# Accumulating DMAs in place of VectorE subtractions for the weight combinations of two down products

## The chip, the cores and the metric

One core of one Trainium2 chip runs the kernel. The metric is device time in microseconds (us) of one execution, and the median of several runs is compared. The engines are TensorE (PE, with its weight loads shown as PEld), VectorE (DVE), ScalarE (ACT), GpSimd (POOL) and SyncE (SP). SP and POOL issue the DMAs of the stage that matters here.

## The reference, cut to what matters

One encoder layer over x of 1024 positions by 1024 channels in float32: a Fourier token mixer, then a gated MLP with a centred convolution over positions, each with adaLN modulation and a layer norm after it. The change touches the last product, the down projection, and its normalization:

```
u = h @ w_up                                   # 1024 x 5632
u = conv over positions (3 taps) + conv_b
val, gate = u[..., :2816], u[..., 2816:]
y = (gelu(gate) * val) @ w_down                # 1024 x 2816 by 2816 x 1024
x = layer_norm(ALPHA * x + g2 * y) * g + b
```

## The kernel before, in words

The down product is done by a scheme of seven half-size products instead of eight (a Strassen-Winograd form). The activations (tensor `gd` in DRAM, 22 tiles of 128 by 1024) are cut into quarters by output rows and by the contraction, the weights `w_down` into quarters W00, W10, W01, W11 (first digit: half of the contraction, second digit: half of the output columns). The products run in the order 1, 2, 5, 6, 3, 7, 4. Each has six blocks `i`: five of two 128-row tiles of the contraction (512 KB of weights) and one of a single tile. So there are 42 steps (p, i).

In each step both operands, an activation block and a weight block, are split into a high and a low part: ACT copies the block to the rounded type fp32r (L53), DVE subtracts that from the block (L54). PE then does three matmuls for each pair of tiles (L284 to L286). The four output row blocks m of a product stand in four PSUM banks and are added into the tiles C when the product ends (`evac`). For the last product `evac` also finishes the four lower row blocks: DVE L821 to L853 with a reciprocal root on POOL (L830 or L840) between, then the store of the row block. `upper_half`, `upper` and `normed` finish the four upper row blocks during products 7 and 4, and their reciprocal root (L426) and their store (L796) are issued on POOL.

The weight operands are made in place by `comb_w` (DVE, L746): for product 5 W01 - W00 in the buffer of W01, for product 6 W11 - (W01 - W00) in the same buffer, for product 7 that minus W00 in the buffer of W00. For product 4 the block W10 is loaded a second time, into the buffer of W11 (tiles `wd_0r` to `wd_10r`), and is subtracted from product 6's combination.

The activation operands are summed partly by accumulating DMAs, issued on POOL (`add_block`, L735): onto `Sg` for products 6 and 3, onto `gr` for product 7.

SP's and POOL's instructions keep the order in which the program writes them. DVE, ACT and PE are ordered by a planner that simulates a timeline with its own costs. The loop over the 42 steps loads 7 steps ahead, issues `add_block` 5 steps ahead, makes combinations 3 steps ahead, and splits 2 steps ahead. The first, second, third and last block of product 4 don't use the shared operand buffers: their parts go to the buffers in the list `fin` (high parts in W00's buffers, low parts in W01's).

Of the kernel before, what the change touches and what calls it, by code (L numbers as in the profile page):

```python
# [11 lines left out]
ALU = mybir.AluOpType  # L12
# [24 lines left out]
def encoder_layer(ctx: ExitStack, tc: tile.TileContext, I, out: bass.AP):  # L37
    nc = tc.nc
    act, dve, pool, pe, sp = nc.scalar, nc.vector, nc.gpsimd, nc.tensor, nc.sync
# [170 lines left out]
    for t, t4 in pairs:  # L210
# [12 lines left out]
        for i, tt in todo:  # L223
            st = sm.tile([128, 2, 6], F32, tag="st", name=f"sta{tt}")
# [204 lines left out]
    for n_t, t in enumerate((1, 2, 0, 3)):  # L429
# [8 lines left out]
        for h in range(2):  # L438
# [15 lines left out]
            for m in range(2):  # L454
                dve.scalar_tensor_tensor(s_[m][:, hs], pb, (-1.0, 1.0)[m], xr[m][:, hs], ALU.mult, ALU.add,
                                         accum_out=sums[m][:, h : h + 1])
        if n_t == 3:
            l_g2 = ada_load(G2)
        for m in range(2):
# [23 lines left out]
            for q in range(2):  # L483
                pt = bank(6 + q, f"tr{nm}_{q}", (4, 128))
                for b in range(4):
                    k = 4 * q + b
                    pe.transpose(pt[:, b, :], hh[:, 128 * k : 128 * k + 128], ident)
                for b in range(4):
                    k = 4 * q + b
# [184 lines left out]
    NK = NB // 2  # L674
# [8 lines left out]
    def w_load(kh, nh, i, slots=None):  # L683
        k, n = PAIRS[i]
        w = slot((slots or bq[kh, nh])[i], [n, 512], F32, f"wd{kh}{nh}_{k}{'r' if slots else ''}")
        r0 = 128 * (NK * kh + k)
        sp.dma_start(w, I["w_down"][r0 : r0 + 128 * n, 512 * nh : 512 * nh + 512].rearrange("(k p) n -> p k n", p=128))
        Bq[kh, nh, i] = w
# [18 lines left out]
    def load_w(p, i):  # L707
        if p in W_OF:
            w_load(*W_OF[p], i)
        elif p == 4:  # L710
            w_load(1, 0, i, bq[1, 1])

    def load_g(p, i):
        if p == 1:
# [23 lines left out]
    def comb_w(p, i):  # L738
        B = {(kh, nh): Bq.get((kh, nh, i)) for kh in range(2) for nh in range(2)}
        if p in (1, 2):  # L740
            return B[p - 1, 0]
        if p == 3:
            return B[1, 1]
        d, x, y = {5: ((0, 1), (0, 1), (0, 0)), 6: ((0, 1), (1, 1), (0, 1)),
                   7: ((0, 0), (0, 1), (0, 0)), 4: ((1, 0), (0, 1), (1, 0))}[p]
        dve.tensor_tensor(B[d], B[x], B[y], ALU.subtract)  # L746
        return B[d]

    def comb_g(p, i):
        r = raw_g.pop((p, i), None)  # L750
# [1 line left out]
            dve.tensor_tensor(Sg[i], Sg[i], r, ALU.add)  # L752
        return Sg[i] if p in (5, 6, 3) else r

    fin = bq[0, 0] + bq[0, 1]

    n_op = [0]

# [39 lines left out]
    def evac(p, m, x):  # L798
        c0, c1 = C[0][m], C[1][m]
        nm = f"f{p}{m}"  # L800
        if p == 1:
            act.activation(c1[:, L], x, AF.Copy, scale=-1.0)
        elif p == 2:
            dve.tensor_tensor(c0[:, L], c1[:, L], x, ALU.subtract)
        elif p == 5:
            act.activation(c1[:, R], x, AF.Copy)
        elif p == 6:
            dve.tensor_tensor(c1[:, L], x, c1[:, L], ALU.add)
            dve.tensor_tensor(c1[:, R], c1[:, R], c1[:, L], ALU.add)
        elif p == 3:  # L810
            dve.tensor_tensor(c0[:, R], c1[:, R], x, ALU.subtract)
        elif p == 7:
            dve.tensor_tensor(c1[:, R], c1[:, R], x, ALU.subtract)
            dve.tensor_tensor(c1[:, L], c1[:, L], x, ALU.subtract)
        else:
            st = st1[m]
            t = slot((33, 34)[m % 2], [512], F32, f"pg{m}")
            n = 512 // x_parts(m)
            rs = sm.tile([128, 1], F32, tag="rs", name=f"rs{nm}")
            if m in sq_rows:  # L820
                dve.tensor_tensor(t, x[0], g2[:, L], ALU.mult)  # L821
                dve.scalar_tensor_tensor(c1[:, L], t, -1.0, c1[:, L], ALU.mult, ALU.add, accum_out=st[:, 0:1])
                nmu = sm.tile([128, 1], F32, tag="nmu", name=f"nmu{nm}")
                dve.tensor_scalar(nmu, st[:, 0:1], st[:, 1:2], -1.0 / D, ALU.add, ALU.mult)
                ss = sm.tile([128, 1], F32, tag="ss", name=f"ss{nm}")
                junk = cp.tile([128, D], mybir.dt.bfloat16, tag="sel", name=f"junk{nm}")
                act.activation(junk, c1, AF.Square, bias=nmu, accum_out=ss)
                ve = sm.tile([128, 1], F32, tag="ve", name=f"ve{nm}")
                dve.tensor_scalar(ve, ss, 1.0 / D, EPS, ALU.mult, ALU.add)
                pool.tensor_tensor(rs, ve, mhalf, ALU.pow)  # L830
            else:
                for k in range(0, 512, n):
                    dve.tensor_tensor(t[:, k : k + n], x[k // n], g2[:, k : k + n], ALU.mult)
                    dve.tensor_tensor(c1[:, k : k + n], c1[:, k : k + n], t[:, k : k + n], ALU.subtract)
                    dve.bn_stats(st[:, k // n, :], c1[:, k : k + n])
                mv = sm.tile([128, 2], F32, tag="mv", name=f"mv{nm}")
                dve.bn_aggr(mv, st)
                ve = sm.tile([128, 1], F32, tag="ve", name=f"ve{nm}")
                dve.tensor_scalar(ve, mv[:, 1:2], EPS, None, ALU.add)
                pool.tensor_tensor(rs, ve, mhalf, ALU.pow)  # L840
                nmu = sm.tile([128, 1], F32, tag="nmu", name=f"nmu{nm}")
                dve.tensor_scalar(nmu, mv[:, 0:1], -1.0, None, ALU.mult)
            nd = D
            lo, hi = slice(0, nd), slice(nd, D)
            if nd < D:
                nb = sm.tile([128, 1], F32, tag="nb", name=f"nb{nm}")
                E(f"nbt{m}").tensor_tensor(nb, nmu, rs, ALU.mult)
                act.activation(c1[:, hi], c1[:, hi], AF.Identity, scale=rs, bias=nb)
                E(f"ng{m}").tensor_tensor(c1[:, hi], c1[:, hi], ffg[:, hi], ALU.mult)
                E(f"nf{m}").tensor_tensor(c1[:, hi], c1[:, hi], ffb[:, hi], ALU.add)  # L850
            if nd:
                dve.scalar_tensor_tensor(c1[:, lo], c1[:, lo], nmu, ffg[:, lo], ALU.add, ALU.mult)
                dve.scalar_tensor_tensor(c1[:, lo], c1[:, lo], rs, ffb[:, lo], ALU.mult, ALU.add)  # L853
            store(1, m)
# [49 lines left out]

    order = (1, 2, 5, 6, 3, 7, 4)
    steps = [(p, i) for p in order for i in range(NP)]
    ready, early, opnd, loaded, added, prepared, split_n = {}, {}, {}, 0, 0, 0, 0
    TAIL = {3: 2, 7: 2, 4: 4}
    acc, late = None, []
    XL = {(7, 5): (1, 0), (4, 0): (1, 1), (4, 1): (1, 2), (4, 2): (1, 3)}  # L910
# [4 lines left out]
    for n, (p, i) in enumerate(steps):  # L915
        while loaded < min(len(steps), n + 7):
            p_, i_ = steps[loaded]
            if p_ != 5:
                load_w(p_, i_)
            load_g(p_, i_)  # L920
            if p_ == 2:
                load_w(5, i_)
            loaded += 1
        while added < min(len(steps), n + 5):
            add_block(*steps[added])
            added += 1
        if 5 <= n < 5 + NP:
            early[5, n - 5] = comb_w(5, n - 5)
        while prepared < min(len(steps), n + 3):
            st_ = steps[prepared]  # L930
            ready[st_] = comb_g(*st_), early.pop(st_) if st_ in early else comb_w(*st_)
            prepared += 1
        if (p, i) in UL:
            xu_load(*UL[p, i])
        if (p, i) in U0:
            upper_half(U0[p, i], 0)
        if (p, i) in XL:
            x_load(*XL[p, i])
        if i == 0:
            acc = [[xbank(f"o{p}_{m}{c}")[:, : 512 // n] for c in range(n)]  # L940
                   for m, n in enumerate(x_parts(m) if p == 4 else 1 for m in range(4))]
            late = []
        if (p, i) == (7, 1):
            ffg = slot(25, [D], F32, "ffg")
            sp.dma_start(ffg, I["ffn_g"])
            ffb = slot(26, [D], F32, "ffb")
            sp.dma_start(ffb, I["ffn_b"])
        if p == 4 and 0 <= i - 1 < 4:
            lower(i - 1)
        while split_n < min(len(steps), n + 2):  # L950
            opnd[steps[split_n]] = operands(*steps[split_n], ready.pop(steps[split_n]))
            split_n += 1
        late.append((PAIRS[i], opnd.pop((p, i))))
        if (p, i) in U1:
            upper_half(U1[p, i], 1)
            upper(U1[p, i])
        tail = TAIL.get(p, 0)
        if i < NP - max(tail, 1):
            todo, final = [late.pop()], False
        elif i == NP - 1:  # L960
            todo, final = late, True
        else:
            continue
        for m in range(4):
            ms = slice(128 * m, 128 * m + 128)
            w = 512 // len(acc[m])
            for c, a in enumerate(acc[m]):
                cs = slice(w * c, w * c + w)
                for (k, kn), (gh, gl, wh, wl) in todo:
                    for q in range(kn):  # L970
                        hl3(a, gh[:, q, ms], gl[:, q, ms], wh[:, q, cs], wl[:, q, cs], k + q == 0, k + q == NK - 1)
            if final:
                evac(p, m, acc[m] if p == 4 else acc[m][0])
# [105 lines left out]
```

## Time and profile before

| | |
|---|---|
| median of 3 runs | 871.85 us (869.87 to 873.02) |
| profiled execution | 872.16 us, span 870.4 us, mean granted clock 0.974 |
| busy in the span | PE 798.9 us (92%), DVE 720.4 (83%), ACT 387.8 (45%), POOL 312.9 (36%) |
| DMA | 131.02 MB, mean 151 GB/s |

The span goes from the first to the last instruction on the core; 1.76 us of the profiled execution lie outside it. Busy shares are means over stages with different limits, so the stage of the change, roughly from 620 us on, is read by itself below.

### The profile page before, as it was taken

The page shows a single profiled execution, that of the slowest core. Times are in us where ns is not written, and L with a number is a line of the kernel's source. Part 1 is how long each engine was busy: PE and PEld are TensorE (multiplying, and loading weights), DVE is VectorE, ACT ScalarE, POOL GpSimd, SP SyncE. Part 2 cuts the span into 40 slices and gives each one's busy share as a digit, 9 for nine tenths or more (in the row PEclk, how much of TensorE's full clock was granted, in tenths as well). Part 3 has the DMA queues.
Part 4 walks back from the last instruction along what each step waited for, and adds up shares of the span by engine and source line. Part 5 has one row for each costly group of instructions (what it writes and reads, how often), then busy time and mean ns, then how long its engine had stood idle before and what let it go on. Part 6 is the DMA issues. An engine that isn't in the chain of part 4 may idle for free.

```text
span 870.4 us, 10731 instructions
## 1 busy us (share of the span) xinstructions
PE 798.9 (92%) x3943; PEld 644.0 (74%) x3943; DVE 720.4 (83%) x991; ACT 387.8 (45%) x559; POOL 312.9 (36%) x244
## 2 busy tenths in 40 slices
PE   2699799998979999999999999999999989999990
PEld 1466577877858888888888888888878868887880
DVE  6972857899899999998888888888677795556998
ACT  7442514577454344444444444444454324335612
POOL 4776802498355444334343333431000122301102
PEclk9899899999989999999999999999999999999995
DMA  9658665572112212322212222210598886808703
GB/s 344 252 183 306 248 228 198 178 270 81 49 49 97 98 73 76 116 85 88 73 72 73 98 97 81 89 49 25 186 375 296 279 213 113 157 25 270 261 27 143
DMA packets 49749, 131.02 MB, mean 151 GB/s; under 512 B 5512, under 2 KB 6664, under 8 KB 49696
## 3 DMA queue, kind: packets, MB, share of 16 engines
q1 hardware_dynamic: 41008, 106.47, 34.6%
q0 software_dynamic: 8400, 22.81, 9.8%
q10 hardware_dynamic: 288, 1.05, 0.3%
q8 instruction: 31, 0.51, 0.2%
q14 instruction: 22, 0.18, 0.1%
HBM read 110.39 MB, written 19.92 MB: 150 GB/s over the span
## 4 chain that ended last, share of the span: by engine, by line
PE 54%; DVE 8%; DMA 7%; issue 3%; POOL 1%; SPq 0%; ACT 0%; DVEq 0%; POOLq 0%
PE x L286 14%; PE x L284 14%; PE x L285 14%; PE o L285 4%; PE o L286 4%; PE o L284 4%; DMA gr<-gd 2%; DMA xu<-x1d 2%; DVE d_1l L54 2%; DMA wd<-in_w_down_dram 1%; DVE d_0l L54 1%; DMA wd_2r<-in_w_down_dram 1%; DMA Sg<-gd 1%; DVE C L853 1%; DVE C L883 1%
## 5 line engine op out<-in xcount | busy, mean ns | idle before, releaser
L284 PE MATMUL x<-Hh,a 128*128 128x512 f32 (+2 forms) x416 | 155.8, 378 | 5.3 <-ACT a L53 5.3
L285 PE MATMUL x<-Hl,a 128*128 128x512 f32 (+2 forms) x416 | 156.6, 377 | 3.9 <-DVE Hl L54 3.1
L286 PE MATMUL x<-Hh,a 128*128 128x512 f32 (+2 forms) x416 | 155.8, 375 | 0.0
L285 PE MATMUL o<-d_1l,d_0h 128*128 128x512 f32 (+1 forms) x299 | 115.0, 385 | 6.5 <-DVE d_1l L54 4.3
L286 PE MATMUL o<-d_1h,d_0l 128*128 128x512 f32 (+1 forms) x299 | 114.7, 384 | 0.0
L284 PE MATMUL o<-d_1h,d_0h 128*128 128x512 f32 (+1 forms) x299 | 102.4, 382 | 0.0
L284 PEld LDWEIGHTS x<-Hh,a 128*128 128x128 f32 x416 | 78.7, 191 | 21.2 <-ACT a L53 6.0
L285 PEld LDWEIGHTS x<-Hl,a 128*128 128x128 f32 x416 | 79.0, 190 | 19.2 <-DVE Hl L54 4.4
L53 ACT ACTIVATE a<-S 128x512 fp32r<-128x512 f32 x80 | 50.4, 630 | 95.6 <-PE x L286 87.2
L286 PEld LDWEIGHTS x<-Hh,a 128*128 128x128 f32 x416 | 78.9, 190 | 14.5 <-issue 0.8
L588 POOL DMA_DIRECT2D gd<-ug x20 | 11.4, 569 | 170.2 <-DVE ug L587 170.2
L285 PEld LDWEIGHTS o<-d_1l,d_0h 128*128 128x128 f32 x299 | 56.6, 189 | 18.7 <-DVE d_1l L54 7.7
L54 DVE TENSOR_TENSOR a<-wu,a 128x512 fp32r<-128x512 f32 x60 | 63.6, 1060 | 3.0 <-ACT a L53 3.0
L286 PEld LDWEIGHTS o<-d_1h,d_0l 128*128 128x128 f32 x299 | 56.6, 189 | 10.8
L284 PEld LDWEIGHTS o<-d_1h,d_0h 128*128 128x128 f32 x299 | 56.3, 189 | 11.0
L54 DVE TENSOR_TENSOR a<-S,a 128x512 fp32r<-128x512 f32 x80 | 61.0, 763 | 0.8
L53 ACT ACTIVATE a<-wu 128x512 fp32r<-128x512 f32 x60 | 37.5, 625 | 40.1 <-PE x L286 38.2
L635 POOL TENSOR_TENSOR S<-wu 128x512 f32<-128x512 f32 x20 | 29.8, 1492 | 69.0 <-DVE a L54 60.3
L735 POOL DMA_DIRECT2D Sg<-gd x12 | 13.9, 1239 | 91.6 <-DVE d_0l L54 91.6
L579 DVE SCALAR_TENSOR_TENSOR t<-uv,cw,t 128x1023 f32<-128x1023 f32 x20 | 35.9, 1793 | 11.4 <-ACT t L578 11.3
L636 POOL TENSOR_TENSOR S<-wu,S 128x512 f32<-128x512 f32 x20 | 43.9, 2195 | 0.1
L53 ACT ACTIVATE d_0h<-Sg 128x1024 fp32r<-128x1024 f32 x15 | 15.9, 1062 | 58.1 <-PE o L285 58.1
(341 smaller groups left out, 1944.5 us busy)
## 6 DMA issues: line engine op xcount, KB each, us to landing
aw<-in_ada_w_dram SPq DMA_DIRECT2D x48, 512.0 KB, 6.2
wu<-in_w_up_dram SPq DMA_DIRECT2D x44, 512.0 KB, 3.2
gd<-ug POOLq DMA_DIRECT2D x20, 512.0 KB, 2.9
wd<-in_w_down_dram SPq DMA_DIRECT2D x20, 512.0 KB, 9.7
gr<-gd SPq DMA_DIRECT2D x15, 512.0 KB, 7.6
gA<-gd SPq DMA_DIRECT2D x10, 512.0 KB, 10.7
Sg<-gd POOLq DMA_DIRECT2D x10, 512.0 KB, 6.2
x<-in_x_dram SPq DMA_DIRECT2D x8, 512.0 KB, 6.1
```

Source lines behind the costliest of these rows:

```text
L53: act.activation(hi, src, AF.Copy)
L54: (eng or dve).tensor_tensor(lo, src, hi, ALU.subtract)
L284: pe.matmul(ps_ap, hi_l, hi_r, start=first, stop=False)
L285: pe.matmul(ps_ap, hi_l, lo_r, start=False, stop=False)
L286: pe.matmul(ps_ap, lo_l, hi_r, start=False, stop=last)
L579: dve.scalar_tensor_tensor(tt[:, 1:S], u[:, 0 : S - 1], w[:, 0:1], tt[:, 1:S], ALU.mult, ALU.add)
L588: pool.dma_start(gd[j], gg)
L635: pool.tensor_tensor(S3, A11, A21, ALU.subtract)
L636: pool.tensor_tensor(S4, A12, S2, ALU.subtract)
L735: pool.dma_start(raw_g[p, i] if p == 7 else Sg[i], gd[k0 : k0 + n, :, 512 * mh : 512 * mh + 512].rearrange("k p c -> p k c"), accum_op=ALU ...
L853: dve.scalar_tensor_tensor(c1[:, lo], c1[:, lo], rs, ffb[:, lo], ALU.mult, ALU.add)
L883: E(f"ub{m}").tensor_tensor(c, c, ffb, ALU.add)
```

## The change

The combinations of products 6, 7 and 4 change sign, and two of the three are no longer made by DVE. Product 6 now takes (W01 - W00) - W11, still a DVE subtraction. Product 7's weights are W00 + that, made by a DMA from SBUF to SBUF that accumulates onto W00's buffer. Product 4's weights are W10 + product 6's combination, made by a DMA from DRAM that accumulates onto W01's buffer. These twelve DMAs are issued on POOL by a new function `add_w`, nine steps ahead, behind the same step's `add_block`. The second load of W10 on SP is dropped, the low parts of product 4's operands go to W11's buffers instead of W01's, and the signs in `evac` follow.

```diff
     def load_w(p, i):
         if p in W_OF:
             w_load(*W_OF[p], i)
-        elif p == 4:
-            w_load(1, 0, i, bq[1, 1])
...
-        d, x, y = {5: ((0, 1), (0, 1), (0, 0)), 6: ((0, 1), (1, 1), (0, 1)),
-                   7: ((0, 0), (0, 1), (0, 0)), 4: ((1, 0), (0, 1), (1, 0))}[p]
+        if p == 7:
+            return B[0, 0]
+        if p == 4:
+            return B[0, 1]
+
+        d, x, y = {5: ((0, 1), (0, 1), (0, 0)), 6: ((0, 1), (0, 1), (1, 1))}[p]
         dve.tensor_tensor(B[d], B[x], B[y], ALU.subtract)
         return B[d]
+
+    def add_w(p, i):
+        if p == 7:
+            pool.dma_start(Bq[0, 0, i], Bq[0, 1, i], accum_op=ALU.add)
+        elif p == 4:
+            k, n = PAIRS[i]
+            r0 = 128 * (NK + k)
+            pool.dma_start(Bq[0, 1, i], I["w_down"][r0 : r0 + 128 * n, 0:512].rearrange("(k p) n -> p k n", p=128),
+                           accum_op=ALU.add)
...
-    fin = bq[0, 0] + bq[0, 1]
+    fin = bq[0, 0] + bq[1, 1]
...
-            dve.tensor_tensor(c1[:, L], x, c1[:, L], ALU.add)
+            dve.tensor_tensor(c1[:, L], c1[:, L], x, ALU.subtract)
...
-            dve.tensor_tensor(c1[:, R], c1[:, R], x, ALU.subtract)
-            dve.tensor_tensor(c1[:, L], c1[:, L], x, ALU.subtract)
+            dve.tensor_tensor(c1[:, R], c1[:, R], x, ALU.add)
+            dve.tensor_tensor(c1[:, L], c1[:, L], x, ALU.add)
...
-                dve.scalar_tensor_tensor(c1[:, L], t, -1.0, c1[:, L], ALU.mult, ALU.add, accum_out=st[:, 0:1])
+                dve.scalar_tensor_tensor(c1[:, L], t, 1.0, c1[:, L], ALU.mult, ALU.add, accum_out=st[:, 0:1])
...
-                    dve.tensor_tensor(c1[:, k : k + n], c1[:, k : k + n], t[:, k : k + n], ALU.subtract)
+                    dve.tensor_tensor(c1[:, k : k + n], c1[:, k : k + n], t[:, k : k + n], ALU.add)
...
+        while added_w < min(len(steps), n + 9):
+            add_w(*steps[added_w])
+            added_w += 1
```

## Rows read from the trace of the kernel before

**Rows 1.** The page's 40 equal slices of the span (21.8 us each), busy tenths of PE and of DVE.

```profile
PE   2699799998979999999999999999999989999990
DVE  6972857899899999998888888888677795556998
```

**Rows 2.** Stretches of the down product: busy us of each engine with its instructions, granted clock, DMA busy share, GB/s.

```profile
720.00:740.00 20.00, 20.00 (x90) 16.57 (x89) 10.68 (x11) 9.02 (x12) 4.69 (x4) 1.00 0.63 103
735.00:775.00 40.00, 40.00 (x178) 33.14 (x177) 22.42 (x24) 15.23 (x16) 8.23 (x7) 1.00 0.57 99
...
785.00:820.00 35.00, 32.89 (x146) 26.89 (x146) 28.40 (x42) 20.93 (x26) 3.65 (x5) 1.00 0.95 315
800.00:820.00 20.00, 20.00 (x91) 16.54 (x90) 20.00 (x30) 13.21 (x18) 2.08 (x2) 1.00 0.97 359
820.00:840.00 20.00, 20.00 (x107) 17.24 (x106) 20.00 (x30) 7.30 (x9) 1.23 (x2) 1.00 0.14 55
840.00:860.00 20.00, 8.23 (x50) 7.19 (x48) 20.00 (x43) 4.86 (x7) 2.58 (x4) 0.81 0.08 33
```

**Rows 3.** The chain of work that ended last, from 600 us on: start, us, what.

```profile
789.37 10.32 DMA wd_2r<-in_w_down_dram
...
858.55 0.57 POOL out_dram L796
859.14 1.13 POOL rsf L830
...
865.40 1.28 DVE C L853
```

**Rows 4.** DVE in order of time around the start of product 7: start, us, line, operation, tiles, shape, and in brackets the idle time before it and what ended it.

```profile
791.72 0.69 DVE L866 SCALAR_TENSOR_TENSOR C<-xu,C 128x512 f32<-128x512 f32 x1 [2.69 <-DMA xu<-x1d]
...
795.78 1.23 DVE L746 TENSOR_TENSOR wd_0r<-wd,wd_0r 128x1024 f32<-128x1024 f32 x1 [3.11 <-DMA wd_0r<-in_w_down_dram]
796.92 1.22 DVE L54 TENSOR_TENSOR d_0l<-gr,d_0h 128x1024 fp32r<-128x1024 f32 x1
798.06 1.22 DVE L54 TENSOR_TENSOR d_1l<-wd,d_1h 128x1024 fp32r<-128x1024 f32 x1
...
799.71 1.23 DVE L746 TENSOR_TENSOR wd_2r<-wd,wd_2r 128x1024 f32<-128x1024 f32 x1 [0.37 <-DMA wd_2r<-in_w_down_dram]
```

**Rows 5.** The instructions of the line that makes the combinations, L746: duration in ns as minimum, median and maximum, first and last start.

```profile
L746 DVE TENSOR_TENSOR wd<-wd,wd x18: 684/1220/1229, 643.7 to 721.1; 128x1024 f32<-128x1024 f32 x15, 128x512 f32<-128x512 f32 x3
...
L746 DVE TENSOR_TENSOR wd_0r<-wd,wd_0r x1: 1226/1226/1226, 795.8 to 795.8; 128x1024 f32<-128x1024 f32 x1
...
L746 DVE TENSOR_TENSOR wd_10r<-wd,wd_10r x1: 684/684/684, 819.2 to 819.2; 128x512 f32<-128x512 f32 x1
```

**Rows 6.** PE in order of time: the first matmul behind its gap in product 7, and its last matmul of the kernel.

```profile
799.33 0.50 PE L285 MATMUL o<-d_1l,d_0h 128*128 128x512 f32 x1 [2.11 <-DVE ve_fn L424]
...
847.96 0.28 PE L286 MATMUL o<-d_1h,d_0l 128*128 128x256 f32 x1
```

**Rows 7.** DVE in order of time during product 4: the last combination, the split behind it, and the first work on the last row block of the last product.

```profile
819.22 0.68 DVE L746 TENSOR_TENSOR wd_10r<-wd,wd_10r 128x512 f32<-128x512 f32 x1
819.83 1.22 DVE L54 TENSOR_TENSOR d_0l<-gA,d_0h 128x1024 fp32r<-128x1024 f32 x1
...
851.01 0.73 DVE L833 TENSOR_TENSOR pg<-o,g 128x256 f32<-128x256 f32 x2
```

**Rows 8.** POOL in order of time: its accumulating DMAs (L735) and the stores of the first two upper row blocks (L796).

```profile
733.46 1.19 POOL L735 DMA_DIRECT2D Sg<-gd  x1 [6.97 <-DVE d_0l L54]
...
744.34 2.12 POOL L735 DMA_DIRECT2D Sg<-gd  x2 [4.25 <-DVE d_0l L54]
745.63 5.74 POOL L735 DMA_DIRECT2D gr<-gd  x4
...
791.63 0.91 POOL L735 DMA_DIRECT2D gr<-gd  x1 [6.52 <-DMA gr<-gd]
...
811.12 0.61 POOL L796 DMA_DIRECT2D out_dram<-C  x1 [11.13 <-DVE C L883]
...
826.01 0.59 POOL L796 DMA_DIRECT2D out_dram<-C  x1 [10.68 <-DVE C L883]
```

**Rows 9.** ACT in order of time: the split of product 3's single block, the next split, the first split of product 7, and the last weight split of product 4.

```profile
755.55 0.63 ACT L53 ACTIVATE d_0s<-Sg 128x512 fp32r<-128x512 f32 x1 [0.94 <-PE o L286]
...
760.76 1.06 ACT L53 ACTIVATE d_0h<-Sg 128x1024 fp32r<-128x1024 f32 x1 [4.06 <-PE o L285]
...
777.08 1.06 ACT L53 ACTIVATE d_0h<-gr 128x1024 fp32r<-128x1024 f32 x1 [3.43 <-PE o L285]
...
833.15 0.62 ACT L53 ACTIVATE d_1h<-wd_10r 128x512 fp32r<-128x512 f32 x1
```

**Rows 10.** SP's queue in order of time: the last activation loads of product 7 (six issues, the last one at 787.3) and the first second load of W10.

```profile
704.86 82.80 SPq L695 DMA_DIRECT2D gr<-gd  x6
...
788.39 0.42 SPq L687 DMA_DIRECT2D wd_0r<-in_w_down_dram  x1
```

**Rows 11.** The accumulating DMAs of `add_block`, L735: time on POOL in ns as minimum, median and maximum, first and last start, and the time from issue to landing.

```profile
L735 POOL DMA_DIRECT2D Sg<-gd x12: 1188/1197/1422, 684.3 to 745.0; - x12
L735 POOL DMA_DIRECT2D gr<-gd x6: 909/2329/3604, 745.6 to 791.6; - x6
...
DMA to landing us min/median/max: 5.4/6.8/14.8
```

More of the change, by code (lines that the diff above doesn't have):

```diff
@@ L906, in encoder_layer @@
     steps = [(p, i) for p in order for i in range(NP)]
-    ready, early, opnd, loaded, added, prepared, split_n = {}, {}, {}, 0, 0, 0, 0
+    ready, early, opnd, loaded, added, added_w, prepared, split_n = {}, {}, {}, 0, 0, 0, 0, 0
     TAIL = {3: 2, 7: 2, 4: 4}
```

## The prediction

> **What bounds the kernel now.** I read the page's slices first. PE is full nearly everywhere and DVE is far from full in most of the down product, but in the last slices it turns round: PE falls to nothing while DVE still stands at 9 [rows 1]. The table of stretches makes that sharp. From 720 to 775 us PE has no gap and DVE idles for close to half of the time; from 800 to 860 us DVE is busy for 60 of 60 us, and from 840 on PE has only 8.23 us of work [rows 2]. PE's last matmul ends at 848.2 us [rows 6], and DVE's last instruction ends 18.4 us later, at 866.7 [rows 3]; the store of the row block fills the remaining 3.7 us of the span. The chain of waits says the same: in its last stretch it goes through DVE, back to a 10.32 us DMA of the reloaded W10 at 789.37 [rows 3]. So in this stage PE is the limit up to about 790 us and DVE from there to the end. Work taken from DVE counts only if it is taken behind 790.
>
> **The change part by part.** *Product 7's combinations off DVE.* Of the 18 combinations that ended by 722.3 us [rows 5], six belong to product 7. Their removal is worth nothing: what DVE is spared there it has as idle time right behind, and between 720 and 775 us PE never waits [rows 2].
>
> *Product 4's combinations off DVE.* Five of 1.22 us and one of 0.68 [rows 5], between 795.8 and 819.9. Successive DVE instructions overlap a little, so I count the distance to the next start: 795.78 to 796.92 is 1.14 [rows 4], and 819.22 to 819.83 is 0.61 [rows 7]. That makes 5 x 1.14 + 0.61 = 6.3 us, all in a stretch where DVE is the limit. This is the main term.
>
> *The second load of W10 off SP's queue.* Its first block can't be issued before 788.39, behind the last of product 7's activation loads, which wait for their buffers [rows 10]. With it go the two waits of DVE on it, 3.11 and 0.37 us [rows 4], together 3.5. Behind the first one stood the split of product 7's third block, which ended at 799.2 for a PE that had run dry: its gap of 2.11 us [rows 6] goes too, so PE's last matmul moves to about 846.1. How much of the 3.5 DVE keeps is open. From 792.7 it has the two splits of that block, 2.3 us, and then needs activation blocks and residual rows that are loaded in a stretch where the DMA engines are 0.95 busy [rows 2]. It can be all, if these come in time, or nothing, if another arrival blocks DVE in the same place, as the residual row did for 2.69 us just before [rows 4]. I take half, 1.7.
>
> *The buffers.* Low parts of product 4's first blocks no longer wait for later combinations to give up W01's buffers: the third block's split stands right behind the last combination now [rows 7]. W11's buffers are free once product 3 is split, so this only helps; I count nothing, because DVE was busy all that time.
>
> *The signs* cost nothing: the same instructions on the same tiles.
>
> *Twelve more DMAs on POOL.* The nearest rows are the accumulating DMAs that are there: 1.20 us of POOL's time for those onto Sg, up to 3.60 for those onto gr, landing in 5.4 to 14.8 us, 6.8 in the median [rows 11]. By order of issue, product 7's six start behind the accumulation at 733.46 and alternate with `add_block`'s; product 4's first two follow among those of 745.63, the third just ahead of the accumulation at 791.63, the fourth behind it [rows 8]. The fifth stands behind the first upper row block's store (811.12) and the sixth behind the second's (826.01) [rows 8], since `upper` is written between them.
>
> What the DMA engines need: from 720 to 740 us, where accumulations make the traffic, 0.63 x 20 = 12.6 us of all engines moved 103 x 20 = 2.06 MB [rows 2], so about 3.2 us for each 512 KB. Product 7's six (5.5 blocks) want 17.6 us and product 4's first two 6.4. From 735 to 775 the engines are busy for 0.57 x 40 = 22.8 us [rows 2]; with 24 more they are full and spill over 775 a little. Who waits? Product 3's single block: its activations, accumulated last in the group at 744.34 [rows 8], now stand behind three weight accumulations. I put its landing at 736 + 5.5 x 3.2 + 3.6 (the median landing less the transfer) = 757. ACT wants it at 755.55, and its next split is due at 760.76 with some 2 us to spare before PE notices [rows 9]. That holds. Product 7's first block is wanted at 777.08 [rows 9] and its eight transfers (7.5 blocks) end near 764. Both ends: a transfer inside SBUF might cost as little as no time beside the others, which changes nothing, or several times 3.2 us, which is the slower rival below.
>
> The last ones: the sixth lands at 826.6 + 1.2 + 6.8 = 834.6 even if the store comes no earlier than now, and the split that wants it stands at 833.15 before and is followed by a DVE backlog [rows 9]. The store should come earlier, so I count nothing.
>
> **The sum.** 872.16 (the profiled execution) - 6.3 - 1.7 = 864.2. The median of the runs is 0.3 below the profiled one, so I forecast 864.0. The lower bound of this case is all 3.5 plus the 2.69, 872.16 - 6.3 - 3.5 - 2.7 = 859.7; the upper bound is the 6.3 less what the order takes back, in the first rival.
>
> **The rivals.** *PE's end holds DVE.* DVE's order is planned. If it keeps its place for the last row block, whose second half starts at 851.4 now [rows 7], DVE can't pass PE's last matmul: at 846.1 that is a gain of 5.3, 866.9; at 848.2, if PE's gap stays, 3.1, 869.1. Against it speaks that of the 15.3 us of DVE behind 851.4 only some 4.3 belong to the last row block; the rest can be put before it.
>
> *A fuller gain.* If the planner finishes three row blocks before PE ends, what is left is the last one's chain of some 4.3 us and a store of 3.7: a span of 854, 856 in all. DVE's remaining work speaks against it: 795.8 to 866.7 less some 0.7 of idling and the 6.3 is 64 us, and from 792.7 on it ends near 856.7 even without idling, which gives a span of 860.4 and 862.
>
> *No change.* The reciprocal roots of the lower row blocks are issued on POOL behind all four upper stores: 858.55, 859.14, then DVE [rows 3]. The fifth and sixth accumulations now stand in that chain. If it isn't shortened by the relief of DVE, its two issues cost 2 x 1.2 = 2.4, 874.6, and at 3.6 us each 7.2, 879.4. For it speaks that the chain's last links stand on the path now; against it, that most of its length is waiting for DVE.
> The Trainium skill speaks for a high price (SBUF — State Buffer, section "SBUF: two separate sides"): descriptors of a DMA issued on GpSimd are written by it, and it is shut out of a shared port while DVE runs in its two-port modes; the page's section "A bandwidth-pool intuition that's wrong (but worth ruling out)" has such a DMA take about 3100 ns instead of 620. By that ratio an issue of 1.2 us would be an estimated 6, and 9.6 us more on this chain. The trace doesn't bear it out: the accumulations onto Sg never took over 1.42 us [rows 11].
>
> *Slower: transfers inside SBUF are dear.* At c us for each 512 KB, product 3's single block lands at 747.6 + 3c. PE waits once that passes about 762.5, c = 5; the gain of 8 is used up at c = 7.6 and at three times the row, 9.6, PE is 14 late and the kernel takes about 878. Nothing in the trace shows such a transfer.
>
> **How the numbers follow.** The forecast (861 to 867) 0.54; PE's end holds DVE (867 to 869.2) 0.17; a fuller gain (856 to 861) 0.08; no change 0.12; slower 0.09. A measurement tells about 0.3% from no change, 2.6 us: below 869.2 is faster, above 874.5 slower. So faster 0.79, same 0.12, slower 0.09. The range that leaves out about 2 in 10 is 858.5 to 870.5.
>
> **What would show it.** Right: DVE's combinations of product 4 gone between 795 and 820, no PE gap near 797, PE's last matmul at 845 to 847, DVE's last instruction at 857 to 861, the stores of the upper rows several us earlier. Wrong: PE idle between 756 and 790 behind a split of product 3 or 7 that waits for a DMA; DVE idle for many us behind 793; POOL issues of 3 us and more behind 800; or the last two weight splits of product 4 waiting for their accumulation, with PE idle behind 830.

## The result, and the profile after

The changed kernel takes 867.57 us in the median of six runs (866.47 to 868.73), against 871.8 for the kernel before (869.87 to 873.95, six runs). The ratio is 0.995, with a 95% interval of 0.9937 to 0.9963: a gain of 4.2 us, about half of the 7.8 that were forecast (871.8 - 864.0), and inside the range. The profiled execution took 866.72 us, of which the span is 864.9 (before: 872.16 and 870.4).

The page's 40 slices, PE and DVE, of the changed kernel:

```profile
PE   2699799997979999999999999999999989999990
DVE  6972857899899999998888888888677784556897
```

Nearly every digit is what it was [rows 1]: at the end of DVE's row only 9 became 8 in the 38th slice (800 to 822 us) and 8 became 7 in the last. Slices of 21.6 us are too coarse for a gain of 4. The table of stretches, changed kernel: length, then the busy us and instructions of PE, PE's weight loads, DVE, ACT and POOL, the granted clock, the DMA engines' busy share and GB/s. The share adds up the times of the packets that start in the stretch, so it can pass 1.

```profile
785.00:820.00 35.00, 35.00 (x157) 28.80 (x156) 26.35 (x41) 21.91 (x26) 8.77 (x9) 1.00 1.01 302
820.00:840.00 20.00, 19.68 (x102) 16.76 (x101) 20.00 (x32) 4.41 (x6) 1.32 (x2) 1.00 0.13 32
725.00:780.00 55.00, 55.00 (x245) 45.54 (x244) 30.14 (x33) 19.57 (x21) 17.42 (x16) 1.00 0.88 161
783.00:861.33 78.33, 60.99 (x298) 51.16 (x296) 68.82 (x113) 32.50 (x40) 17.73 (x17) 0.91 0.58 175
```

And two stretches of the kernel before that answer to the last two; the second runs from the start of product 7 (to within 0.1 us of its first matmul) to DVE's end, as 783.00 to 861.33 does after.

```profile
725.00:780.00 55.00, 55.00 (x244) 45.57 (x243) 29.13 (x32) 21.92 (x26) 10.62 (x9) 1.00 0.49 84
785.36:866.68 81.32, 60.76 (x298) 51.03 (x296) 74.61 (x119) 32.73 (x40) 10.66 (x13) 0.91 0.52 181
```

The last pair holds most of the account. Behind the start of product 7, DVE has six instructions fewer and 74.61 - 68.82 = 5.8 us less to do. But the stretch became only 81.32 - 78.33 = 3.0 us shorter, because DVE's idle time grew from 6.7 to 9.5 us. Of the relief, 2.8 us went into new waiting, although the waits for the reloaded W10 are gone.

The spans differ by more, 5.5 us, because product 7 starts 2.4 us earlier in this execution. Of that, 1.8 us is there at the first matmul of the down product already. PE in order of time, before:

```profile
629.23 0.39 PE L284 MATMUL o<-d_1h,d_0h 128*128 128x512 f32 x1
```

and after:

```profile
627.39 0.39 PE L284 MATMUL o<-d_1h,d_0h 128*128 128x512 f32 x1
```

Up to there both programs give every engine the same instructions in the same order, so these 1.8 us are not the change's. Another 0.5 us comes up between that matmul and product 7, where a PE gap in product 5 is shorter (3.25 us, before 3.88), and 0.15 in the last store. Without the 1.8 the two profiles differ by 3.7 us, which fits the 4.2 of the medians (interval 3.2 to 5.5).

Where DVE waits now: DVE in order of time, changed kernel (in brackets the idle time before the instruction and what ended it).

```profile
785.45 1.22 DVE L54 TENSOR_TENSOR d_1l<-wd,d_1h 128x1024 fp32r<-128x1024 f32 x1
792.01 0.69 DVE L877 SCALAR_TENSOR_TENSOR C<-xu,C 128x512 f32<-128x512 f32 x1 [5.35 <-DMA xu<-x1d]
...
804.06 0.69 DVE L877 SCALAR_TENSOR_TENSOR C<-xu,C 128x512 f32<-128x512 f32 x1 [0.75 <-DMA xu<-x1d]
...
847.48 0.74 DVE L844 TENSOR_TENSOR pg<-o,g 128x256 f32<-128x256 f32 x2
```

DVE's waits by what ended them, changed kernel from 782 us on: us in total, times, the longest.

```profile
DVE C L877 <- DMA xu<-x1d: 6.1, 2, 5.3
DVE nbfn L891 <- POOL rs_fn L426: 1.1, 3, 0.5
DVE C L893 <- ACT C L892: 1.0, 1, 1.0
```

The waits for the reloaded W10 (3.11 and 0.37, together 3.5) went, but the wait for the residual row ahead of them, 2.69 before [rows 4], is 5.35 now, 2.7 more. The rest of the idle time, 6.7 - 2.7 - 3.5 = 0.5 us before, is 9.5 - 5.35 = 4.1 us now, in small waits of under 1 us each: for another residual row, for POOL's reciprocal roots, for ACT. So 3.5 went and 6.3 came. SP's queue and POOL hold a possible reason. SP, changed kernel:

```profile
785.63 0.33 SPq L797 DMA_DIRECT2D xu<-x1d  x1
```

POOL in order of time, changed kernel:

```profile
781.43 1.19 POOL L733 DMA_DIRECT2D gr<-gd  x1 [24.80 <-DVE C L876]
782.13 1.71 POOL L757 DMA_DIRECT2D wd<-in_w_down_dram  x1
791.45 0.88 POOL L733 DMA_DIRECT2D gr<-gd  x1 [7.61 <-DMA gr<-gd]
...
807.33 0.61 POOL L807 DMA_DIRECT2D out_dram<-C  x1 [7.72 <-DVE nmufu L881]
...
817.29 0.61 POOL L807 DMA_DIRECT2D out_dram<-C  x1 [6.83 <-DVE C L894]
```

And before, POOL and SP:

```profile
783.91 1.19 POOL L735 DMA_DIRECT2D gr<-gd  x1 [32.54 <-DMA gr<-gd]
...
788.00 0.33 SPq L786 DMA_DIRECT2D xu<-x1d  x1
```

The residual row's load is issued 2.4 us earlier than before (785.63, where it was 788.00), but two accumulations were issued 3.5 and 4.2 us ahead of it, where before there was one, 4.1 us ahead; and it takes 6.4 us to arrive instead of 3.7, counted to the DVE instruction that it releases. So the row comes at 792.0 in the one kernel and at 791.7 in the other: DVE reaches its place earlier and waits longer. That the accumulations ahead are the cause was a reading of order at this point; the experiments take it up.

### The profile page after: what moved, and what is told of

Read it like the earlier page. It is cut to its first block, busy times and chain, and to the rows that moved or that the text cites. A ratio compares the mean times of both kernels' runs of the same rounds, so it can differ in the third digit from the quotient of the medians.

```text
span 864.9 us, 10742 instructions
## 1 busy us (share of the span) xinstructions
PE 799.9 (92%) x3943; PEld 644.2 (74%) x3943; DVE 708.3 (82%) x979; ACT 387.3 (45%) x559; POOL 328.9 (38%) x256
## 4 chain that ended last, share of the span: by engine, by line
PE 57%; DVE 6%; DMA 6%; issue 2%; POOL 1%; ACT 1%; SPq 0%; POOLq 0%; ACTq 0%; DVEq 0%
PE x L286 14%; PE x L284 14%; PE x L285 14%; PE o L285 5%; PE o L286 5%; PE o L284 5%; DMA gr<-gd 2%; DMA xu<-x1d 2%; DMA wd<-in_w_down_dram 1%; DVE d_1l L54 1%; DVE d_0l L54 1%; DMA Sg<-gd 1%; DVE C L864 1%; POOL S L635 0%; DVE C L894 0%
## 5 line engine op out<-in xcount | busy, mean ns | idle before, releaser
L54 DVE TENSOR_TENSOR d_1l<-wd,d_1h 128x1024 fp32r<-128x1024 f32 (+1 forms) x37 | 44.0, 1189 | 0.0
```

The source lines that it names most:

```text
L54: (eng or dve).tensor_tensor(lo, src, hi, ALU.subtract)
```

## The experiments

Five questions: which of the two products brings the gain (the first two runs and a mended one); what DVE's relief and the spared load are worth each by itself (three runs); whether the residual row took the missing half (two); whether the late accumulations did (two); and whether a plain earlier load would have done as well as an accumulation (two). All ratios are against the kernel before, run beside them (medians 871.49 to 871.91).

**Product 7's part alone.** Product 4 goes back to a second load of W10 and DVE's combination (with the sign that goes with the negated W01), and its low parts go to W01's buffers.

```
 load_w:  +        elif p == 4:
          +            w_load(1, 0, i, bq[1, 1])
 comb_w:  -        if p == 4: return B[0, 1]
          +        4: ((1, 0), (0, 1), (1, 0)) with ALU.add
 add_w:   only p == 7
```

> The changed kernel, but product 4's weights are made as before: W10 is loaded a second time and DVE adds product 6's combination; only product 7's weights come from the accumulating DMAs inside SBUF. Theory A (the gain comes from product 4's six DVE instructions, which stood where DVE sets the end; product 7's stood where DVE has idle time): no gain, 870.5 to 872.5 us against some 871.8 for the kernel before. Rival B (product 7's part carries the gain, since DVE is relieved before product 6 too): 868 us or below. Rival C (the transfers inside SBUF cost something that product 4's part had to pay for): 873 us or above.

871.15 us; ratio 0.9995 (0.9981 to 1.0009). Product 7's combinations come off DVE where DVE idles, and it is worth nothing, as costed.

**Product 4's part alone, first form.** Product 7 is combined on DVE again.

```
 comb_w:  -        if p == 7: return B[0, 0]
          +        7: ((0, 0), (0, 1), (0, 0)) with ALU.add
 add_w:   only p == 4
```

> The changed kernel, but product 7's weights are made by DVE as before (an addition, the signs are the changed kernel's); only product 4's come from accumulating DMAs. Theory A: the whole gain, 866.5 to 868.5 us. Rival B (product 7's part carries it): 870 to 872 us. Rival C (the transfers inside SBUF cost something): under 866 us.

884.11 us; ratio 1.0146 (1.0126 to 1.0165). A miss, and by the way the kernel was written: each accumulation onto W01's buffer stands ahead of the DVE combination of product 7 that reads the same buffer, so that combination takes W01 with W10 already added, and has to wait for the DMA. Four of product 7's six combinations waited; DVE in order of time:

```profile
761.09 1.23 DVE L746 TENSOR_TENSOR wd<-wd,wd 128x1024 f32<-128x1024 f32 x1 [6.12 <-DMA wd<-in_w_down_dram]
...
797.86 1.22 DVE L746 TENSOR_TENSOR wd<-wd,wd 128x1024 f32<-128x1024 f32 x1 [4.71 <-DMA wd<-in_w_down_dram]
...
825.44 1.23 DVE L746 TENSOR_TENSOR wd<-wd,wd 128x1024 f32<-128x1024 f32 x1 [3.12 <-DMA wd<-in_w_down_dram]
...
827.78 0.69 DVE L746 TENSOR_TENSOR wd<-wd,wd 128x512 f32<-128x512 f32 x1 [1.04 <-DMA wd<-in_w_down_dram]
```

This kernel doesn't tell what was asked, but it prices something else: a DVE instruction that stands behind such an accumulation waits for it, 15.0 us in four waits here, and with it all of DVE's queue. The change has no such place, because nothing on DVE but a split reads an accumulated block.

**Product 4's part alone, mended.** As above, with the accumulations written behind the combinations:

```
-        while added_w < min(len(steps), n + 9): ...   (ahead of the prepared loop)
+        while added_w < min(len(steps), n + 9): ...   (behind it)
```

> Product 7's weights by DVE, product 4's by accumulating DMAs, as in e2_p4_only, but with each accumulation written behind the making of product 7's combination, so that DVE's addition no longer waits for a DMA and reads the buffer before W10 is added. Theory A: the whole gain of the change, 866.5 to 868.5 us. If the transfers inside SBUF (absent here) cost something in the changed kernel: under 866.5 us. If product 7's part is needed for the gain: 869.5 us or above.

869.13 us; ratio 0.9966 (0.995 to 0.9982). With the 0.05% of product 7's part that makes 0.4%, against 0.5% for the change: the two parts add up within their intervals. The time itself lies between the forecasts, 0.6 us above the one for the whole gain. The first residual row, SP and DVE:

```profile
788.97 0.33 SPq L793 DMA_DIRECT2D xu<-x1d  x1
...
795.12 0.69 DVE L873 SCALAR_TENSOR_TENSOR C<-xu,C 128x512 f32<-128x512 f32 x1 [5.10 <-DMA xu<-x1d]
```

The long wait for the residual row is there without the transfers inside SBUF. Product 4's accumulations from DRAM are enough for it.

**DVE's relief alone.** The kernel before with product 4's six subtractions left out; the second load of W10 stays, so product 4 multiplies by W10 instead of the difference.

```
+        if p == 4:
+            return B[1, 0]
```

> The kernel before without product 4's six subtractions: the reloaded block W10 alone stands as its weights, so the output isn't the reference's; all loads and the buffers stay. Theory A (DVE's work is what counts): about the changed kernel's time, 866.5 to 869 us. Rival D (the second load of W10 with its two waits is what counts, 3.5 us of them on DVE): about the kernel before, 870.5 to 872 us, since the weights still arrive as late.

866.38 us; ratio 0.9938 (0.9921 to 0.9954), a gain of 5.1 us, with the load as late as before. The stretch from product 7's start to DVE's end:

```profile
785.80:862.30 76.50, 60.79 (x298) 51.06 (x296) 68.55 (x113) 32.51 (x40) 14.28 (x13) 0.92 0.55 193
```

and DVE's waits:

```profile
DVE C L868 <- DMA xu<-x1d: 3.8, 2, 2.5
DVE d_1l L54 <- ACT d_1h L53: 2.6, 1, 2.6
```

DVE has 68.55 us of work, as after the change, but 8.0 us of idle time instead of 9.5, in a stretch that is 1.8 shorter. The late load still costs DVE 2.6 us, by way of ACT's split of it, and the residual row 2.5. The changed kernel doesn't have the first and pays 5.35 for the second, 2.8 more: as the two traces read, what the spared load gave was lost at the residual row. The two kernels' times differ by 1.2 us (866.38 and 867.57), which their intervals don't settle.

**The spared load alone, first form.** The kernel before without the second load; product 4 subtracts from W11, which is resident, instead.

```
-        elif p == 4:
-            w_load(1, 0, i, bq[1, 1])
-        4: ((1, 0), (0, 1), (1, 0))
+        4: ((1, 1), (0, 1), (1, 1))
```

> The kernel before without the second load of W10: product 4's six subtractions take the block W11 that is in the buffer, so the output isn't the reference's; DVE's work and the buffers stay. Theory A: little, 869.5 to 871.5 us, because the waits of 3.5 us on the load go but DVE still has the 6.3 us. Rival D (the load counts): the changed kernel's time or better, 868.5 us or below.

866.25 us; ratio 0.994 (0.9922 to 0.9958). A miss, and the trace says why. The combinations' line:

```profile
L744 DVE TENSOR_TENSOR wd<-wd,wd x24: 684/1220/1227, 645.0 to 776.5; 128x1024 f32<-128x1024 f32 x20, 128x512 f32<-128x512 f32 x4
```

All 24 combinations are over by 776.5. With its operand resident the planner moved product 4's six ahead of product 7, into DVE's idle time, so this kernel too takes 6 us off DVE where DVE is the limit. It repeats the run before it (0.9938), and says nothing of the load by itself. But it shows that DVE's own combinations, with their operand there early enough, cost no more than leaving them out.

**The spared load alone, second form.** The load is left out and the six subtractions are held back by an operand that comes late: each subtracts the same step's activation block, in place of W10's.

```
-        raw_g[p, i] = g_load(1, 1, i, block(i, (1, 0), "gA22_"))
+        raw_g[p, i] = Bq[1, 0, i] = g_load(1, 1, i, block(i, (1, 0), "gA22_"))
-        4: ((1, 0), (0, 1), (1, 0))
+        4: ((1, 1), (0, 1), (1, 0))
```

> The kernel before without the second load of W10, but with product 4's six subtractions kept in their late place: they subtract the activation block of the same step, which is loaded there anyway, so the output isn't the reference's. Theory A (the place of DVE's work counts, the load by itself little): 869 to 871.5 us. Rival D (the load counts): 867 us or below, like e4_no_load.

870.14 us; ratio 0.999 (0.9976 to 1.0003). DVE in order of time, the first and the last of the six:

```profile
793.86 1.23 DVE L744 TENSOR_TENSOR wd<-wd,gA 128x1024 f32<-128x1024 f32 x1 [1.26 <-DMA gA<-gd]
...
813.17 0.68 DVE L744 TENSOR_TENSOR wd<-wd,gA 128x512 f32<-128x512 f32 x1
```

Now they stand where they stood; the first one waits 1.26 us for the activation block, where it waited 3.11 for W10. The load's absence is worth 0.9 us by the ratio, 1.8 by the medians, 2.1 by the interval's lower end (0.0024 x 871.9), and nothing by its upper one. The 1.7 that the prediction took for it lies inside; so does zero.

**The residual row early.** In the changed kernel, two of the upper half's residual rows are loaded in product 3, ahead of the accumulations, instead of in products 3 and 7.

```
-    UL = {..., **{((7, i) if i else (3, 5)): (i, 1) for i in range(4)}}
+    UL = {..., (3, 2): (0, 1), (3, 3): (1, 1), (7, 2): (2, 1), (7, 3): (3, 1)}
```

> The changed kernel, with the second halves of the residual rows of the upper row blocks 0 and 1 loaded during product 3 (steps (3, 2) and (3, 3)) instead of behind product 7's activation loads. Theory E (what DVE was spared was partly given back as idle time: 5.35 us at 786.7 to 792.0 until that residual row came, and some 3 us until 820 behind the late chain of the upper rows): most of the 5.35 comes back, 861.5 to 864.5 us. Rival F (that idle time costs nothing, because DVE's order is bound by PE's results of product 7 and 4 anyway): 866.5 to 868.5 us, no change against the changed kernel.

865.46 us; ratio 0.9925 (0.9908 to 0.9942): 2.1 less than the change, half of what was hoped. The 5.35 us wait is gone, and another has come into its place. DVE in order of time:

```profile
796.58 0.16 DVE L891 TENSOR_TENSOR nbfn<-nmufu,rs_fn 128x1 f32<-128x1 f32 x1 [3.26 <-POOL rs_fn L426]
```

POOL in order of time, the same kernel:

```profile
793.84 0.88 POOL L733 DMA_DIRECT2D gr<-gd  x1 [7.43 <-DVE d_0l L54]
794.39 1.57 POOL L757 DMA_DIRECT2D wd<-in_w_down_dram  x1
795.12 1.43 POOL L426 TENSOR_TENSOR rs_fn<-ve_fn,mhalf 128x1 f32<-128x1 f32 x1
```

The row block's reciprocal root (L426), whose input DVE had written at 786.7, is issued behind two accumulations on POOL, the first of which waited 7.43 us for a DVE split. DVE, a few instructions on, waits for that root.

**The same edit in the kernel before.**

> The kernel before with the same earlier load of the two residual rows. Theory E: DVE waits 2.69 us for the row before, but 3.11 us for the reloaded weights stand right behind it and are not touched: a gain of 0 to 3, 869 to 872 us. Rival F: no change, 871 to 872.5 us. If it gains as much as in the changed kernel (5 us), the residual row was a limit of its own and the change's relief has nothing to do with it.

869.98 us; ratio 0.9973 (0.9959 to 0.9988). It gains about as much without the change (0.27%) as with it (0.25%). So the residual row is a limit of its own in both kernels, and the part of the missing gain that is the change's doing can't be read from this edit. DVE's wait behind it, for the reload, is 3.5 us there, as before.

**Product 4's accumulations earlier.** Twelve steps ahead instead of nine.

```
-        while added_w < min(len(steps), n + 9):
+        while added_w < min(len(steps), n + (9 if added_w < 36 else 12)):
```

> The changed kernel, with product 4's accumulating DMAs written twelve steps ahead instead of nine, so that none stands behind a store of an upper row block or behind product 7's last activation accumulations on POOL. Theory E: the third one no longer runs beside the residual row's load at 785.6, which landed after 6.3 us instead of 3.7: up to 2.6 us less, and ACT's wait of 1.37 us on the last but one goes: 865 to 867.5 us. Rival G (POOL's queue with the stores sets the end): 863 us or below. If the DMA engines, full from 741 to 775 us, only spill further: 867.5 us or above.

867.73 us; ratio 0.9953 (0.9938 to 0.9968): no gain on the change. DVE's waits from 782 us on:

```profile
DVE C L877 <- DMA xu<-x1d: 7.7, 3, 3.1
```

The first of the three, DVE in order of time:

```profile
790.20 0.69 DVE L877 SCALAR_TENSOR_TENSOR C<-xu,C 128x512 f32<-128x512 f32 x1 [3.12 <-DMA xu<-x1d]
```

With no accumulation issued in the 20 us ahead of its load (786.03), the first residual row arrives after 4.2 us, and the wait for it is 3.1 us instead of 5.35. But the edit moved the activation accumulation of 781.43 as well (to 786.45, behind that load), so by itself it doesn't say which of the two accumulations had lengthened the way. The other traces do. In the five kernels that had only the activation accumulation ahead of that load, by 4.1 to 4.3 us, the row came after 3.6 to 4.2 us: 3.7 in the kernel before, 4.2 with product 7's part alone, 3.6 without the subtractions, 4.0 and 4.1 without the load. In the two that had one of product 4's accumulations 3.5 us ahead too, it came after 6.4 (the change) and 6.2 (product 4's part, mended). So the weight accumulation lengthens the way by some 2 to 3 us. What that costs in time is not shown: two later rows are now waited for by 1.9 and 2.7 us, where the changed kernel has one wait of 0.75, and PE shows gaps of 2.2 and 2.8, so nothing is won in sum. The edit doesn't clear the place either; the sixth weight accumulation now stands there, at 787.17, just ahead of the second row's load (787.41).

**Both edits.**

> The changed kernel with both edits, the residual rows' earlier load and product 4's accumulations twelve steps ahead. If the two cures are independent, the gains add: 860 to 864 us. If both only cure the same wait, no better than the earlier load alone.

864.23 us (862.39 to 865.93); ratio 0.9914 (0.9897 to 0.9931). DVE's waits from 782 us on:

```profile
DVE C L877 <- DMA xu<-x1d: 3.1, 2, 1.8
DVE nbfn L891 <- POOL rs_fn L426: 2.2, 2, 1.8
```

This is the best median: 7.5 us below the kernel before and 3.3 below the change, with intervals that don't touch. From the early rows alone (865.46) it isn't told apart: those intervals overlap. Against the kernel before with the same residual rows early (0.9973), the accumulations are worth 0.59%, 5.1 us, and by the two intervals some 3 to 7. That fits what the relief of DVE alone brought (5.1), as it should with the rows and the accumulations out of each other's way, but it doesn't show that as the cause.

**A plain load, early.** The kernel before; W10's second load is issued at step 28 in one piece, ahead of the next load of activations, and DVE goes on subtracting.

```
-        elif p == 4:
-            w_load(1, 0, i, bq[1, 1])
...
+        if n == 28:
+            for k in range(NP):
+                w_load(1, 0, k, bq[1, 1])
```

> The kernel before, complete, without accumulations onto weights, with W10's second load written on SP ahead of product 7's fifth activation load, so that it arrives from 750 us on and DVE can make product 4's combinations in its idle time before 785. Theory A: DVE is relieved as in the changed kernel, and no accumulation disturbs the loads at 785: 865.5 to 867.5 us, as good as the change or better. If accumulating by DMA is what brings the gain: 870 us or above.

871.26 us; ratio 0.9994 (0.9978 to 1.001): nothing. DVE's waits from 755 us on:

```profile
DVE wd_0r L744 <- DMA wd_0r<-in_w_down_dram: 2.6, 1, 2.6
DVE wd_8r L744 <- DMA wd_8r<-in_w_down_dram: 2.5, 1, 2.5
...
DVE wd_6r L744 <- DMA wd_6r<-in_w_down_dram: 2.0, 1, 2.0
DVE wd_4r L744 <- DMA wd_4r<-in_w_down_dram: 1.6, 1, 1.6
```

and the stretch from 755 to 788:

```profile
755.00:788.00 33.00, 30.90 (x137) 25.23 (x136) 23.45 (x26) 9.91 (x11) 0.21 (x1) 1.00 0.54 144
```

SP's waits from 700 to 800 us, and the residual row's load:

```profile
SPq L687 <- DVE d_1l L54: 70.7, 5, 43.4
...
793.38 0.42 SPq L784 DMA_DIRECT2D xu<-x1d  x1
```

The subtractions are now planned into product 3, where DVE has time to spare, but they stand in its queue ahead of splits, and DVE waits 8.7 us for their blocks. PE, which in the kernel before is busy for all 33.00 us of this stretch, loses 33.00 - 30.90 = 2.1 us. Behind product 7's start the stretch to DVE's end became 3.0 us shorter (78.30, before 81.32); most of that was paid back here.

The blocks came late for a reason that the forecast overlooked. W10 goes into W11's buffers, and W11 is product 3's weight block, so SP waits for product 3's splits, block by block: the six loads are issued from 750.94 to 780.70. What stands behind them on SP comes later too, the residual row's load at 793.38 instead of 788.00. So this run shows what the load costs in this place, and not what an early operand is worth. The nearest to that is the run with the resident operand (0.994), which has no load at all and gained as much as the change. The accumulating DMA has two things over this load: W01's buffers are free earlier (with the accumulations written earlier, five of the six were issued by 765), and nothing but a split waits for it.

**The plain early load with the early residual rows.**

> e10_early_load with the residual rows' earlier load of e5_early_xu as well. If the two waits at the start of product 7 are separate, 862 to 865.5 us, at least as good as e8_both (864.2); if DVE's backlog behind product 7 alone sets the end, 865.5 us or above.

868.13 us; ratio 0.996 (0.9946 to 0.9974), 2.7 us more than the change with the same rows early (865.46). The second forecast came true in its number; the loads wait for W11's buffers here too, so it says no more of the mechanism than the run before.

## Why the prediction was right, and which term was off

The time lies in the range, with 4.2 us of the 7.8 that were forecast. The place of the gain was right; the sum was too large.

**Product 7's part, nothing.** Right, in a run of its own (0.9995).

**Product 4's combinations, 6.3.** Right in place and nearly in size: 5.8 us less of DVE's work behind product 7's start in the trace, and 5.1 us of time where the six were left out and nothing else was changed.

**The waits on the reloaded W10, half of 3.5.** This is the mis-sized term. Counted at 1.7 us of gain, DVE's waits came out in the changed kernel's profile at 2.8 of loss (idle 6.7 to 9.5): the 3.5 did go, but 2.7 came at the residual row and 3.6 in small waits behind it. The prediction's own lower end for it was nothing, "if another arrival blocks DVE in the same place, as the residual row did for 2.69 us just before"; that arrival did block it, and the end was not low enough. The price that was left out is that of new transfers on a load that DVE waits for; the sum has no term for it. The prediction had the order of product 4's third accumulation right, just ahead of the activation accumulation that was at 791.63, but took from it no time: POOL was free and issued it at 782.13, 9.3 us ahead of that one, and the residual row's load, issued 3.5 us behind it, took 2.7 us longer than before. Writing it earlier gave back 2.2 us at that place, and nothing in the sum. Of the sum, 5.8 - 2.8 = 3.0 is what the trace has behind product 7's start; with the 0.5 at product 5 and the 0.15 in the store it is the 3.7 named above. The runs by themselves say the same less sharply: DVE's relief brought 5.1 us and the spared load 0.9, together 6.0, and the change 4.2; with intervals of 1.1 to 1.5 us either way for each, the 1.8 between them isn't settled.

**The DMA price, 3.2 us for 512 KB.** Right. From 725 to 780 us the DMA engines were busy 0.88 x 55 = 48.4 us after and 0.49 x 55 = 27.0 before: 21.4 more for 7.5 blocks, 2.9 each. Product 3's single block came in time: ACT in order of time, changed kernel,

```profile
753.19 0.63 ACT L53 ACTIVATE d_0s<-Sg 128x512 fp32r<-128x512 f32 x1 [0.94 <-PE o L286]
...
819.27 1.06 ACT L53 ACTIVATE d_1h<-wd 128x1024 fp32r<-128x1024 f32 x1 [1.37 <-DMA wd<-in_w_down_dram]
```

it starts 2.4 us earlier than before and still waits for PE alone, by the same 0.94 us [rows 9]. The second line is the one place where ACT waits for an accumulated weight block, 1.37 us, and PE has 0.32 us of idle time in the stretch that follows. So the slower rival (dear transfers inside SBUF) is out; its own price is measured in the last section.

**PE's gap near 797.** Gone: PE is busy for 35.00 of the 35 us from 785 to 820, where it was 32.89 [rows 2]. PE's last matmul, put at 845 to 847, starts at 844.03 and ends at 844.31; 1.8 us of its lead are older than the down product, and without them it ends at 846.1, as forecast.

```profile
844.03 0.28 PE L286 MATMUL o<-d_1h,d_0l 128*128 128x256 f32 x1
```

**The other signs.** DVE's last instruction was put at 857 to 861. It ended at 861.33, and without the 1.8 us it would be 863.2: a miss. Two of the signs of being wrong came in a small way: DVE idles for 4.0 us behind 793, in pieces of under 1 us, and the last but one weight split of product 4 waits 1.37 us for its accumulation, with 0.32 us of idle PE behind 830. The other two didn't come.

**The rivals.** "PE's end holds DVE" had the right time (866.9 to 869.1) and the wrong mechanism: DVE starts on the last row block at 847.48, 3.2 us behind the end of PE's last matmul, and from 813 us on it waits for PE nowhere. "No change" fell: the upper rows' stores moved forward (811.12 to 807.33, 826.01 to 817.29 [rows 8]) and POOL's chain came with them. The estimate of 6 us for an issue while DVE runs, worked out from the Trainium skill (SBUF — State Buffer, section "A bandwidth-pool intuition that's wrong (but worth ruling out)"), didn't come: product 4's issues behind 800 took 1.23 and 0.91 us. That page of the Trainium skill has its figures from a DMA beside a DVE `tensor_copy`. What DVE ran beside these two issues were splits (TENSOR_TENSOR), so the page's own case was not tried here. POOL's queue can hold DVE all the same, by order and not by the price of an issue: most in the kernel with the early residual rows (3.26 us), and 1.8 us with both edits.

**What stays open.** The 1.2 us between the change and the run with the subtractions left out lie inside their intervals; the trace puts them at the residual row, which is a reading. Why the residual rows that follow are late when product 4's accumulations come earlier was not tried further. And no run has a plain early load of W10 into buffers that are free, so whether it would do as well as the accumulation is open.

## What to carry to other kernels

Work taken off an engine that runs in order is worth what it costs only as far as the next entry of that engine's queue is ready; look at the wait just behind the place, and ask what the DMA that replaces the work does to the load that ends it. An accumulating DMA takes more off the engine than the operation: it takes the wait for the operand out of its queue too. Before a load is written earlier, ask when its buffer comes free; the plain load tried here waited for that, and everything behind it in its queue with it. Move the loads that the engine waits for next ahead of the new traffic in the same step. Here that brought the gain from 0.5% to 0.75%, and 0.86% with the accumulations issued earlier too; but 0.27% was to be had by that move without the change.

## What the runs showed of the hardware

The accumulating DMAs, changed kernel: time on POOL in ns as minimum, median and maximum, first and last start. Those inside SBUF, and those from DRAM:

```profile
L753 POOL DMA_DIRECT2D wd<-wd x6: 1420/1762/3896, 731.8 to 746.4; - x6
...
L757 POOL DMA_DIRECT2D wd<-in_w_down_dram x6: 914/1397/2215, 750.5 to 817.9; - x6
```

The two runs that have one kind each give their price. The stretch from 725 to 780 us with product 7's part alone (six inside SBUF, 5.5 blocks), and with product 4's part, mended (two from DRAM):

```profile
725.00:780.00 55.00, 55.00 (x245) 45.54 (x244) 29.13 (x32) 20.89 (x24) 15.45 (x15) 1.00 0.76 135
...
725.00:780.00 55.00, 55.00 (x244) 45.54 (x244) 29.13 (x31) 22.83 (x27) 13.06 (x11) 1.00 0.61 104
```

The kernel before has a share of 0.49 there. So the first kind took (0.76 - 0.49) x 55 = 14.9 us of all DMA engines, 2.7 for each 512 KB, and the second (0.61 - 0.49) x 55 = 6.6 us, 3.3 each. An accumulation of one SBUF block onto another was about as dear as one from DRAM; with shares in hundredths, which are 0.55 us, the difference is not to be leant on.

The time on POOL goes by the place in the queue and not by the kind. Inside SBUF it is 1.42 to 1.44 us for the first three and rises to 3.90 for the last of a group that is issued back to back; with product 4's part, mended, two from DRAM in such a group took 3.61 and 4.63 us.

And an accumulation issued just ahead lengthened the way of a load in another queue: the residual row's, of 256 KB, took 6.2 and 6.4 us with a weight accumulation 3.5 us ahead of it, and 3.6 to 4.2 in the five kernels that had only an activation accumulation there.
